# Four weight fusions in the opening of a gMLP and pooling backbone, with hand-placed side steps and four staging tiles

## The chip, the cores and the metric

The kernel runs on one core of a Trainium2 chip. The metric is device time in microseconds, from the first to the last instruction of the program and the little that lies around them; lower is better. Every program here is one launch, and all data starts and ends in the chip's main memory (HBM).

## The reference

Two layers work on 2048 latent tokens of width 1024, in float32. Each layer normalises its rows, scales and shifts them by an adaLN vector that is computed from a condition `c` and a weight `ada_w`, mixes them, and adds a gated residual. Layer 0 is a chunked gMLP, layer 1 a multi-scale centred pooling. Cut to what matters:

```python
shift, scale, gate = split(silu(c) @ ada_w[i] + ada_b[i], 3)
h = rmsnorm(x, norm_g[i]) * (1 + scale) + shift
# layer 0
u, v, g = split(h @ gmlp_w_in, 3)
s = einsum(w_s, layernorm(gelu(v))) + b_s        # over chunks of 128 tokens
y = (gelu(u) * s * silu(g)) @ gmlp_w_out
# layer 1
p, g = split(h @ pool_w_in, 2)
pooled = [centred_mean(p_k, w_k) - p_k for w_k in (2, 4, 8, 16)]
y = (einsum(pooled, pool_w_grp) * scale * silu(g)) @ pool_w_out
x = x + gate * y                                  # and a last rmsnorm
```

In layer 1 the pooling acts on tokens and `pool_w_grp` on channels, so the product of the first half of `pool_w_in` with `pool_w_grp` can be formed once, ahead of the rows. The kernel does so: this is the weight fusion, one 1024x512 product for each of the four windows (groups g = 0 to 3).

## The kernel before

Rows lie transposed (channels on partitions) in blocks of 512 tokens; two blocks make a pair. Big products use a seven-product scheme of the Strassen kind over quarters of weights and rows. Every float32 operand is split into a high and a low part (`put`, L108: a ScalarE copy for the high part, a VectorE subtraction for the low one), and each product is three matmuls (`mm3`, L102). One such split costs one instruction on each of the two engines.

Weights come through one stream (`Stream`, L33): a list of jobs, each with a load on SyncE's DMA queue into one of six `raw` tiles of 512 KB and a split. `st.get(i)` first issues loads for up to four jobs beyond the ones being split, and splits up to `st.ahead` jobs beyond i. The jobs are listed once at the start (L354 to L371), so their order in the list is the order of the loads.

The fusion of a group is `fuse(g)` (L705). It has two halves (kh), each with four steps (cc) of 12 matmuls into four accumulators `pf`; after each step it runs some steps of the side work. At the end of a half four copies on ScalarE (L716) bring the accumulators into staging tiles, and GpSimd's queue writes each to `wf_d` in HBM (L717), 256 KB a write. The staging tile is `t2`, a tag with two buffers, which the weight jobs also use for sums of quarters. The tag `s` has four buffers; its other users are the fourth quarter of the gMLP's v weights (`sixth`, L261), the gMLP's spatial results, and rows of the output phases.

The opening runs `fuse(0)`, `fuse(1)` and `fuse(2)`, and beside them a queue `side` of small steps: `ada`, ten steps that load eight rows of `ada_w` of 1 MB each (tag V, four buffers, of which one is the sum), accumulate them on VectorE (L446, L448), and end in small matmuls on TensorE (`pm`, L454) that give the scale and shift; `rs`, eleven steps that load the first 512 rows of x, square and sum them and end in their norm (`pss` L495, `pr` L519); `steps`, the same for the second 512 rows, which stay in eight of the nine `g` tiles; `halfs`, nine steps that modulate the first 512 rows and split them; and `late`, twelve steps that modulate the second 512 rows and form the sums of quarters that the seven products need, and four more (`late[1]`) for the last of these sums.

Side work is handed out by count: `do_side((2, 3, 3, 2)[g])` after each fusion step (L713). What is left after the third fusion runs in a loop of its own down to nine steps (L809), and the rest inside `v_phase(0)`, the first phase of the gMLP. `v_phase` takes its products in the order 1, 2, 6, 7, 5, 3, 4 (VORDER); 1 and 2 need the first 512 rows alone, 6 needs a sum from `late`. It hands out two side steps a slot in its first eight slots, in both calls (L859).

The fourth fusion, `fuse(3)`, runs later, between `b_phase0(0)` and `c_phase0(0)` (L1004), with the first nine steps of `sum_steps` (the rows of the next pair) beside it. In `v_phase(1)` the side work is `tsum`: for each of eight column blocks, reads of `wf_d` into x, x, ra and th, four VectorE sums (L736 to L739), and writes to `t_d`.

Instructions of an engine and of a DMA queue run in the order in which the program holds them; that order is made ahead of time by a planner that takes work whose buffers and inputs it expects to be ready, with the order of the source as priority. A `load` is held behind the last stream load that was listed before it (L127).

Of the kernel before, what the change touches and what calls it, by code (L numbers as in the profile page):

```python
# [22 lines left out]
TB = 512  # L23
# [40 lines left out]
def hybrid_kernel(ctx: ExitStack, tc: tile.TileContext, a: dict):  # L64
# [26 lines left out]
    def work(tag, width=512):  # L91
        return wk.tile([P, WK[tag][0]], F32, name=tag, tag=tag, bufs=WK[tag][1])[:, 0:width]
# [20 lines left out]
    side = deque()  # L113

    def do_side(n=1000):
        for _ in range(min(n, len(side))):
            side.popleft()()
# [110 lines left out]
    def fusion_jobs(g):  # L228
        rhs, lhs = [], [[], []]
        for kh in range(2):  # L230
            for cc in range(4):
                if kh == 0 and cc % 2 == 0:
                    rhs += halves(lambda cc=cc: a["pool_grp"][g, cc // 2], 512 if g == 0 and cc == 0 else W2)
                lhs[kh].append(half_job(lambda kh=kh, cc=cc: a["pool_wpT"][g, cc, :, kh * 512:kh * 512 + 512]))
        return rhs, lhs
# [115 lines left out]
            ws[1] += w(c, 1)  # L351
        return ys, ws

    jf = [fusion_jobs(g) for g in range(3)]  # L354
    jv, jug, jc0 = [], [], []
    for b in (0, 2):
        jv.append(v_jobs())
        jug.append(ug_jobs())
        if b == 0:
            jf.append(fusion_jobs(3))  # L360
        jc0 += [c0_jobs(b), c0_jobs(b + 1)]

    def pg_jobs():
# [167 lines left out]
    def src0(b):  # L531
        return lambda d: a["xT"][d, :, b * TB:(b + 1) * TB]
# [172 lines left out]
    def fuse(g):  # L705
        for kh in range(2):
            pf = [bank("pf") for _ in range(4)]
            for cc in range(4):
                x = st.get(rhs_lhs(g)[0][cc])
                w = st.get(rhs_lhs(g)[1][kh][cc])  # L710
                for k in range(4):
                    mm3(pf[k], part(w, every, slice(k * P, (k + 1) * P)), x, cc == 0, cc == 3)
                do_side((2, 3, 3, 2)[g])  # L713
            for kk in range(4):
                t = work("t2")
                nc.scalar.copy(t, pf[kk])  # L716
                nc.gpsimd.dma_start(  # L717
                    wf_d[(g % 2) * 4:(g % 2) * 4 + 4, kh, :, g // 2, kk, :].rearrange("j p n -> p j n"),
                    t.rearrange("p (j n) -> p j n", j=4))
# [31 lines left out]
    xbig, xb = [], []  # L751
# [9 lines left out]
    def bias_steps():  # L761
# [8 lines left out]
        def make(q):  # L770
# [4 lines left out]
            for i in range(2):  # L775
                for g in range(2):
# [11 lines left out]
    ada = ada_steps(0, 0, 16, lambda: bigtile("V", F32, "araw"), lambda: bigtile("V", F32, "aacc"))  # L788
    rs = rms0[0].steps(row_start)
    rows = Rows(0, [src0(0), src0(1)], rms0)  # L790
    others = []
    rms, steps = fetched_rms(src0(1), TB, "ra", "x", 2, others)
    rms0.append(rms)
    side.extend([ada[0], rs[0], rs[1], ada[1], rs[2], rest, ada[2], rs[3], rs[4], ada[3], rs[5], rest, ada[4], rs[6], rs[7], rest, ada[5],
                 rest, ada[6], rs[8], rest, ada[7], rs[9], rest, ada[8], rs[10], ada[9]])
    halfs = rows.half_steps(0, xb)
    two_ways = deque(steps)
    for f in halfs:
        side.append(f)
        for _ in range(2):  # L800
            if two_ways:
                side.append(two_ways.popleft())
    side.extend(two_ways)
    late = rows.rest_steps(xb, others)
    side.extend(late[0])

    for g in range(3):
        fuse(g)
    while len(side) > 9:  # L809
        do_side(1)  # L810


    def v_phase(pb, rows):

        st.ahead = 0
        bst = sp.tile([P, 8, 4, 6], F32, name="bst", tag="bst", bufs=1)

        def finish(i, n, t, src):

            nc.scalar.activation(t, src, AF.Gelu_apprx_tanh)  # L820
            nc.vector.bn_stats(bst[:, i, n, :], t)
            nc.gpsimd.dma_start(v_d[pb, 2 * n:2 * n + 2, :, i, :].rearrange("c p n -> p c n"),
                                t.rearrange("p (c n) -> p c n", c=2))

        for n in range(2):
            pa = [bank("pa") for _ in range(4)]
            pv = {}
            o = {}
            for pn in VORDER:
                idx, x = jv[pb][n][pn], rows.operand(NAME[pn])  # L830
                for t in range(4):
                    if pn in (1, 6, 7, 4):
                        p, onto = pa[t], pn != 1
                    else:
                        onto = pn == 3
                        if not onto:
                            pv[t] = bank("pv")
                        p = pv[t]
                    for k in range(4):
                        mm3(p, part(x[k], every, slice(t * P, (t + 1) * P)), st.get(idx[k]), k == 0, k == 3, onto)  # L840
                    st.make()
                    if pn in (1, 6, 5):
                        o[t, pn] = work("g")
                        nc.scalar.copy(o[t, pn], p)
                    elif pn == 2:
                        nc.vector.tensor_add(o[t, 1], o[t, 1], p)
                        finish(t, 2 * n, o[t, 1], o[t, 1])
                        if t == 3:
                            pv = {}
                    elif pn == 3:  # L850
                        nc.vector.tensor_add(o[t, 6], o[t, 6], p)
                        finish(t, 2 * n + 1, o[t, 6], o[t, 6])
                    elif pn == 4:
                        u = work("g")
                        finish(4 + t, 2 * n, u, p)
                    if pn == 5:
                        nc.vector.tensor_add(o[t, 5], o[t, 5], pa[t])
                        finish(4 + t, 2 * n + 1, o[t, 5], o[t, 5])
                    do_side(2 if n == 0 and pn < 3 else 1)  # L859
        mv = sp.tile([P, 8, 2], F32, name="mv", tag="mv", bufs=1)  # L860
        for i in range(8):
            nc.vector.bn_aggr(mv[:, i, :], bst[:, i].rearrange("p a b -> p (a b)"))
        ve, rs, rt, sh = (sp.tile([P, 8], F32, name=nm, tag=nm, bufs=1) for nm in ("ve", "rs", "rt", "sh"))
        nc.vector.tensor_scalar_add(ve, mv[:, :, 1], EPS)
        rsqrt(rs, ve, rt)
        nc.vector.scalar_tensor_tensor(sh, mv[:, :, 0], -1.0, rs, ALU.mult, ALU.mult)
        return mv, rs, sh
# [127 lines left out]
    for b in (2, 3):  # L995
        rms, steps = fetched_rms(src0(b), TB, "ra", "x", 5)
# [4 lines left out]
    rows = Rows(0, [src0(2), src0(3)], rms0)  # L1001
    sums = rows.sum_steps(lambda: work("g"))
    side.extend(sums[:9])
    fuse(3)  # L1004
    c_phase0(0)
    side.extend(sums[9:])
    c_phase0(1)
# [7 lines left out]
    for b in (0, 1):  # L1015
        rms, steps = fetched_rms(src1(b), TB, "ra", "x", 8)
# [4 lines left out]
    rows = Rows(1, [src1(0), src1(1)], rms1)  # L1021
# [115 lines left out]
    for b in (2, 3):  # L1137
        rms, steps = fetched_rms(src1(b), TB, "ra", "x", 8)
# [5 lines left out]
    rows = Rows(1, [src1(2), src1(3)], rms1)  # L1144
# [32 lines left out]
    for j, (t0, n) in enumerate(LAST):  # L1177
# [3 lines left out]
        rms = Rms(n, "ra", "x")  # L1181
# [79 lines left out]
```

## Time and profile before

| | us |
|---|---|
| median of three runs | 2511.09 |
| lowest and highest of them | 2510.03 and 2515.03 |
| the profiled execution | 2508.11 |
| its span | 2506.3 |

The rows below come from the one profiled execution. Times in them are microseconds from the start of its span. A timeline row gives the start, the length, the engine, the line and the operation with its tiles (written before, read behind the arrow); in brackets stands how long the engine was idle before it and what released it. PE is TensorE, PEld its weight loads, DVE VectorE, ACT ScalarE, POOL GpSimd, SPq the DMA queue of SyncE. The granted TensorE clock is given as a share of 2.4 GHz, so 0.50 is 1.2 GHz.

### The profile page before, as it was taken

The page shows a single profiled execution, that of the slowest core. Times are in us where ns is not written, and L with a number is a line of the kernel's source. Part 1 is how long each engine was busy: PE and PEld are TensorE (multiplying, and loading weights), DVE is VectorE, ACT ScalarE, POOL GpSimd, SP SyncE. Part 2 cuts the span into 40 slices and gives each one's busy share as a digit, 9 for nine tenths or more (in the row PEclk, how much of TensorE's full clock was granted, in tenths as well). Part 3 has the DMA queues.
Part 4 walks back from the last instruction along what each step waited for, and adds up shares of the span by engine and source line. Part 5 has one row for each costly group of instructions (what it writes and reads, how often), then busy time and mean ns, then how long its engine had stood idle before and what let it go on. Part 6 is the DMA issues. An engine that isn't in the chain of part 4 may idle for free.

```text
span 2506.3 us, 32884 instructions
## 1 busy us (share of the span) xinstructions
PE 2439.6 (97%) x11392; PEld 2054.6 (82%) x11392; DVE 1919.3 (77%) x3207; ACT 1038.4 (41%) x1833; POOL 258.7 (10%) x481
## 2 busy tenths in 40 slices
PE   6789999999999989999999999999999999999998
PEld 5668888888788878888888888888888888888998
DVE  5686788998854667888897737999885498999655
ACT  4554544333643434443335533333264333333533
POOL 2111100000100342000000001110000001010001
PEclk8799999999999999999999999999999999999999
DMA  9433434454755675343455645333367545354764
GB/s 351 162 114 120 152 113 139 154 168 137 247 192 187 213 251 183 113 130 123 137 160 189 216 158 172 125 110 113 108 211 230 161 138 189 117 168 136 251 194 146
DMA packets 170966, 418.43 MB, mean 167 GB/s; under 512 B 21408, under 2 KB 45984, under 8 KB 169776
## 3 DMA queue, kind: packets, MB, share of 16 engines
q1 hardware_dynamic: 138960, 314.01, 39.4%
q0 software_dynamic: 27808, 97.57, 10.7%
q10 hardware_dynamic: 4032, 4.75, 0.7%
q8 instruction: 90, 1.47, 0.2%
q14 instruction: 76, 0.62, 0.1%
HBM read 327.16 MB, written 89.10 MB: 166 GB/s over the span
## 4 chain that ended last, share of the span: by engine, by line
PE 61%; issue 23%; DVE 8%; DMA 5%; POOL 2%; ACT 1%; ACTq 0%; POOLq 0%; DVEq 0%; SPq 0%
PE pu L104 11%; PE pu L106 11%; PE pu L105 11%; PE po L104 6%; PE po L106 6%; PE po L105 6%; PE pa L104 2%; PE pa L105 2%; PE pa L106 2%; DVE wlo L111 1%; DMA wf_d<-t 1%; PE psp L899 1%; PE pv L105 1%; PE pv L106 1%; PE pv L104 1%
## 5 line engine op out<-in xcount | busy, mean ns | idle before, releaser
L111 DVE TENSOR_TENSOR wlo<-raw,whi 128x512 fp32r<-128x512 f32 x816 | 549.3, 685 | 266.6 <-ACT whi L110 261.0
L110 ACT CAST whi<-raw 128x512 fp32r<-128x512 f32 x816 | 489.0, 617 | 611.3 <-PE po L105 234.9
L104 PE MATMUL pu<-S,whi 128*128 128x512 f32 x1024 | 400.9, 391 | 0.0
L106 PE MATMUL pu<-S,wlo 128*128 128x512 f32 x1024 | 398.7, 389 | 0.0
L105 PE MATMUL pu<-S,whi 128*128 128x512 f32 x1024 | 398.5, 389 | 0.0
L106 PE MATMUL po<-whi,wlo 128*128 128x512 f32 (+1 forms) x768 | 300.1, 391 | 4.5 <-DVE wlo L111 4.5
L104 PE MATMUL po<-whi 128*128 128x512 f32 (+1 forms) x768 | 299.6, 390 | 1.2 <-ACT whi L110 1.2
L104 PE MATMUL pu<-A,whi 128*128 128x512 f32 x768 | 300.1, 391 | 0.0
L106 PE MATMUL pu<-A,wlo 128*128 128x512 f32 x768 | 299.1, 389 | 0.7 <-DVE wlo L111 0.7
L105 PE MATMUL po<-wlo,whi 128*128 128x512 f32 (+1 forms) x768 | 299.4, 390 | 0.0
L105 PE MATMUL pu<-A,whi 128*128 128x512 f32 x768 | 298.8, 389 | 0.0
L106 PEld LDWEIGHTS pu<-S,wlo 128*128 128x128 f32 x1024 | 192.2, 188 | 40.3
L105 PEld LDWEIGHTS pu<-S,whi 128*128 128x128 f32 x1024 | 192.3, 188 | 39.1
L104 PEld LDWEIGHTS pu<-S,whi 128*128 128x128 f32 x1024 | 192.3, 188 | 39.1
L106 PEld LDWEIGHTS po<-whi,wlo 128*128 128x128 f32 x768 | 144.6, 188 | 36.5 <-DVE wlo L111 6.5
L104 PEld LDWEIGHTS po<-whi 128*128 128x128 f32 x768 | 144.5, 188 | 32.0 <-ACT whi L110 1.8
L106 PEld LDWEIGHTS pu<-A,wlo 128*128 128x128 f32 x768 | 144.2, 188 | 31.3 <-DVE wlo L111 1.1
L105 PEld LDWEIGHTS po<-wlo,whi 128*128 128x128 f32 x768 | 144.5, 188 | 30.2
L104 PEld LDWEIGHTS pu<-A,whi 128*128 128x128 f32 x768 | 144.2, 188 | 29.8 <-ACT whi L110 0.4
L105 PEld LDWEIGHTS pu<-A,whi 128*128 128x128 f32 x768 | 144.2, 188 | 29.7
L105 PE MATMUL po<-big,whi 128*128 128x388 f32 (+1 forms) x384 | 123.1, 321 | 1.9 <-DVE big L111 1.9
L104 PE MATMUL po<-big,whi 128*128 128x388 f32 (+1 forms) x384 | 123.2, 321 | 0.0
(234 smaller groups left out, 4003.5 us busy)
## 6 DMA issues: line engine op xcount, KB each, us to landing
raw<-in_g_wo SPq DMA_DIRECT2D x64, 512.0 KB, 4.4
raw<-in_p_wo SPq DMA_DIRECT2D x96, 256.0 KB, 3.3
v_d<-g POOLq DMA_DIRECT2D x64, 256.0 KB, 2.7
raw<-in_g_wu SPq DMA_DIRECT2D x32, 512.0 KB, 4.0
raw<-in_g_wg SPq DMA_DIRECT2D x32, 512.0 KB, 4.5
raw<-v_d SPq DMA_DIRECT2D x32, 512.0 KB, 4.6
y_d<-s POOLq DMA_DIRECT2D x64, 256.0 KB, 2.7
x<-in_ada_w SPq DMA_DIRECT2D x64, 256.0 KB, 3.0
```

The lines of the kernel that those rows point to most:

```text
L104: nc.tensor.matmul(out, w[0], x[0], start=first and not onto, stop=False, skip_group_check=onto)
L105: nc.tensor.matmul(out, w[0], x[1], start=False, stop=False, skip_group_check=onto)
L106: nc.tensor.matmul(out, w[1], x[0], start=False, stop=last, skip_group_check=onto)
L110: nc.scalar.copy(pair[0], src)
L111: nc.vector.tensor_sub(pair[1], src, pair[0].bitcast(F32))
L899: nc.tensor.matmul(p[:, t * P:(t + 1) * P], vt[h][:, t * 2 * P + j * P:t * 2 * P + (j + 1) * P], bw[:, 0:P], start=True, stop=True)
```

## The change

All four fusions run in the opening, and their jobs stand ahead of everything else in the stream. The side work of the opening is no longer a queue with a count for each fusion but a table of 32 places, one for each fusion step; each side step is put in a place by hand. The staging tile of a fusion's result is `s` (four buffers) in place of `t2` (two). The loop that ran left-over side steps without products beside them is gone; the last three of the twelve `late` steps go to `v_phase(0)`. The pauses in the norm of the second 512 rows go (wait 2 becomes 0). In `v_phase` the pace of two steps a slot holds in the first call alone. `fuse(3)` is no longer between `b_phase0(0)` and `c_phase0(0)`, so the first nine `sum_steps` run inside `c_phase0(0)`.

```diff
-    jf = [fusion_jobs(g) for g in range(3)]
+    jf = [fusion_jobs(g) for g in range(4)]
...
-        if b == 0:
-            jf.append(fusion_jobs(3))
...
-                do_side((2, 3, 3, 2)[g])
+                for f in plan.pop(0):
+                    f()
             for kk in range(4):
-                t = work("t2")
+                t = work("s")
...
-    rms, steps = fetched_rms(src0(1), TB, "ra", "x", 2, others)
+    rms, steps = fetched_rms(src0(1), TB, "ra", "x", 0, others)
...
-    side.extend([ada[0], rs[0], rs[1], ada[1], rs[2], rest, ada[2], rs[3], rs[4], ada[3], rs[5], rest, ada[4], rs[6], rs[7], rest, ada[5],
-                 rest, ada[6], rs[8], rest, ada[7], rs[9], rest, ada[8], rs[10], ada[9]])
+    late = rows.rest_steps(xb, others)
     halfs = rows.half_steps(0, xb)
...
+    plan = [[] for _ in range(32)]
+
+    def place(steps, at):
+        for f, i in zip(steps, at):
+            plan[i].append(f)
+
+    place(rs, (0, 0, 1, 2, 3, 4, 5, 6, 10, 12, 13))
+    place(ada, (1, 2, 4, 6, 8, 10, 12, 14, 16, 18))
+    place(steps, (12, 14, 15, 16, 17, 18, 19, 20, 21, 24, 25, 26))
+    place(halfs, (18, 19, 19, 20, 20, 21, 21, 22, 22))
+    place(late[0], (27, 27, 28, 28, 29, 29, 30, 30, 31))
+    for g in range(4):
         fuse(g)
-    while len(side) > 9:
-        do_side(1)
+    side.extend(late[0][9:])
...
-                    do_side(2 if n == 0 and pn < 3 else 1)
+                    do_side(2 if pb == n == 0 and pn < 3 else 1)
...
     side.extend(sums[:9])
-    fuse(3)
     c_phase0(0)
```

## Rows read from the trace of the kernel before

**Rows 1.** The page: TensorE's busy time, its granted clock in 40 slices.

```profile
PE 2439.6 (97%) x11392; PEld 2054.6 (82%) x11392; DVE 1919.3 (77%) x3207; ACT 1038.4 (41%) x1833; POOL 258.7 (10%) x481
...
PEclk8799999999999999999999999999999999999999
```

**Rows 2.** Windows: length, busy time of each engine, clock, DMA share, GB/s.

```profile
0.00:69.00 69.00, 43.18 (x180) 33.66 (x180) 41.19 (x54) 27.32 (x49) 13.45 (x26) 0.85 0.95 350
20.00:40.00 20.00, 16.13 (x67) 11.87 (x65) 9.48 (x10) 7.14 (x13) 3.00 (x4) 0.96 1.02 399
0.00:152.00 152.00, 111.46 (x459) 89.36 (x460) 102.97 (x164) 78.81 (x140) 24.68 (x41) 0.85 0.62 220
```

**Rows 3.** Timeline of TensorE in the opening and the start of `v_phase(0)`.

```profile
7.38 0.69 PE L104 MATMUL pf<-whi 128*128 128x512 f32 x1 [0.35 <-ACT whi L110]
...
45.44 0.79 PE L104 MATMUL pf<-whi 128*128 128x512 f32 x1 [9.05 <-ACT whi L110]
...
69.18 6.99 PE L454 MATMUL pm<-ones,aacc 128*128 128x1 f32 x32 [10.83 <-DVE aacc L448]
...
111.83 0.39 PE L106 MATMUL pf<-whi,wlo 128*128 128x512 f32 x1
...
114.55 0.39 PE L106 MATMUL pa<-whi,A 128*128 128x512 f32 x1
122.18 1.22 PE L104 MATMUL pa<-whi,A 128*128 128x512 f32 x2 [7.24 <-ACT whi L110]
...
151.71 0.63 PE L104 MATMUL pa<-whi,S 128*128 128x512 f32 x1
```

**Rows 4.** Groups, 0 to 152: busy, mean ns, idle before, its releasers.

```profile
L448 DVE SCALAR_TENSOR_TENSOR aacc<-araw,cond,aacc 128x2048 f32<-128x2048 f32 x7 | 16.4, 2347 | 1.3 <-DMA araw<-in_ada_w 1.3
L716 ACT COPY t<-pf 128x512 f32<-128x512 f32 x24 | 14.0, 583 | 36.4 <-DMA wf_d<-t 30.9 <-PE pf L106 5.4
...
L105 PE MATMUL pv<-wlo,A 128*128 128x512 f32 x12 | 5.7, 475 | 7.3 <-DVE wlo L111 7.3
```

**Rows 5.** The tile wf_d, 0 to 140: landing times of its 24 writes.

```profile
DMA to landing us min/median/max: 2.7/6.3/8.6
```

**Rows 6.** DMA issues, 0 to 40: count, KB each, median us to landing.

```profile
araw<-in_ada_w SPq DMA_DIRECT2D x6, 1024.0 KB, 10.7
raw<-in_pool_wpT SPq DMA_DIRECT2D x15, 256.0 KB, 8.3
```

**Rows 7.** The chain that ended last: the small matmuls of a later adaLN part.

```profile
483.87 0.79 PE pm L454 x8
```

**Rows 8.** Timeline of VectorE: two subtractions and additions back to back.

```profile
118.70 0.68 DVE L582 TENSOR_TENSOR g<-g,rrow 128x512 f32<-128x512 f32 x1
119.30 0.68 DVE L643 TENSOR_TENSOR g<-g 128x512 f32<-128x512 f32 x1
```

**Rows 9.** Timeline around the fourth fusion: ScalarE, then TensorE.

```profile
652.59 0.59 ACT L716 COPY t<-pf 128x512 f32<-128x512 f32 x1 [2.37 <-DMA wf_d<-t]
656.53 1.22 PE L106 MATMUL po<-whi,wlo 128*128 128x512 f32 x2 [3.26 <-DVE wlo L111]
```

**Rows 10.** Windows: the fourth fusion's end, the start of `c_phase0(2)`.

```profile
650.00:660.00 10.00, 6.74 (x24) 5.13 (x23) 6.81 (x12) 6.52 (x13) 3.00 (x4) 0.83 0.67 234
1330.00:1340.00 10.00, 8.82 (x39) 6.84 (x38) 7.07 (x12) 4.47 (x8) 0.54 (x1) 1.00 0.56 147
```

**Rows 11.** Windows in `v_phase(1)`.

```profile
880.00:890.00 10.00, 7.79 (x35) 6.12 (x33) 2.77 (x4) 0.00 (x0) 4.33 (x8) 1.00 0.81 289
890.00:900.00 10.00, 5.29 (x12) 3.70 (x13) 6.99 (x12) 1.79 (x4) 4.00 (x7) 0.59 0.79 254
```

**Rows 12.** Timeline of VectorE in `v_phase(1)`.

```profile
891.55 0.69 DVE L736 TENSOR_TENSOR x<-x 128x512 f32<-128x512 f32 x1 [6.28 <-DMA x<-wf_d]
892.15 1.89 DVE L111 TENSOR_TENSOR wlo<-s,whi 128x512 fp32r<-128x512 f32 x3
```

**Rows 13.** Timeline of SyncE's DMA queue: two issues of adaLN rows.

```profile
38.04 9.65 SPq L128 DMA_DIRECT2D araw<-in_ada_w  x2
```

More of the change, by code (lines that the diff above doesn't have):

```diff
@@ L791, in hybrid_kernel @@
     others = []
-    rms, steps = fetched_rms(src0(1), TB, "ra", "x", 2, others)
+    rms, steps = fetched_rms(src0(1), TB, "ra", "x", 0, others)
     rms0.append(rms)
-    side.extend([ada[0], rs[0], rs[1], ada[1], rs[2], rest, ada[2], rs[3], rs[4], ada[3], rs[5], rest, ada[4], rs[6], rs[7], rest, ada[5],
-                 rest, ada[6], rs[8], rest, ada[7], rs[9], rest, ada[8], rs[10], ada[9]])
+    late = rows.rest_steps(xb, others)
     halfs = rows.half_steps(0, xb)
[L797 to L807, printed above, removed]
+    plan = [[] for _ in range(32)]
[8 more added lines that the diff above has]
+    for g in range(4):
         fuse(g)
-    while len(side) > 9:
-        do_side(1)
+    side.extend(late[0][9:])
     def v_phase(pb, rows):
```

## The prediction

> **What bounds the kernel now.** I read the page first: TensorE is busy for 97% of the span, and its granted clock is below full only in the first slices [rows 1]. So whatever moves the time has to give TensorE back time that it loses, and most of that is lost early. The windows of the opening come next [rows 2], then TensorE's timeline there [rows 3], and last the groups that say what ended the idle time of the other engines [rows 4].
>
> I set the mark at 151.71, where product 6 of `v_phase(0)` starts [rows 3]; until then TensorE should have done three fusions (288 matmuls) and products 1 and 2 (96). Twelve matmuls take 2.72 us from 111.83 to 114.55, 0.2267 us each [rows 3], so these 384 are worth 87.1 us. 151.7 - 87.1 = 64.6 us are spent otherwise. The first 7.4 are the start. The reader should see three kinds in the rest. First, TensorE waits 9.05 us for a weight's high part and later 7.24 us again [rows 3]: ScalarE, which makes these parts, stood in front of a copy L716 that waits for the write of an earlier result to leave its staging tile, 30.9 us in all [rows 4]. A write takes 6.3 us in the median and 8.6 at most [rows 5], and there are two tiles for four results. Second, 10.83 us for the sum of the adaLN rows; the small matmuls `pm` behind it then take 6.99 us, because the clock had fallen (the same kind takes 0.79 us for 8 records at full clock, so 3.2 for 32) [rows 3, 7]. Third, VectorE is late when `v_phase(0)` begins: 7.3 us of waits for low parts in product 2 [rows 4]. After the mark TensorE runs without a gap for a long while.
>
> **The change part by part.** *The fourth fusion moves.* Its 96 matmuls (21.8 us) leave the middle and come before the mark; TensorE's work is the same. With it move 12 splits, 3 MB of loads on SyncE's queue (they no longer stand ahead of the first loads of `c_phase0(0)`), and 8 writes on GpSimd's. Like for like, the mark before counts as 151.7 + 21.8 = 173.5.
>
> *The floors of the new opening.* TensorE: 7.4 + 480 x 0.2267 = 116.2, plus `pm` at full clock 3.2 and the norm's small matmuls, for which I take as much again, 122.6 us. VectorE: 103.0 busy until the mark [rows 2], plus 12 splits at 0.60, the distance of two starts [rows 8]: 110.2; it begins near 6, so 116. DMA: 220 GB/s for 152 us are 33.4 MB [rows 2]; with 5 MB (5.2 million bytes) more, 38.7 MB; at the 399 GB/s of the fullest stretch [rows 2] 97 us. All three lie near each other: the gain is what the order saves of the waits, and the new mark can't come before about 123.
>
> *Four staging tiles.* A half of a fusion lasts 48 x 0.2267 = 10.9 us. Its four writes are out some 4 us after its end and land in 6.3 to 8.6 [rows 5], at 10 to 13 us; the next half asks for the first tile at 11 and for the last at 13. So the copy's wait falls to between 0 and 1 us; I take 0. The `s` loads of v weights (1 MB) now wait for the last writes of the fusion, until 10 to 13 us after its end; with a landing like the other weights' 8.3 us at worst [rows 6] they are there at 18 to 21, and product 6 starts at 21.8 and wants four VectorE operations (2.4 us) first. Cost 0 to 2, I take 0; no load for products 1 and 2 stands behind them on SyncE's queue.
>
> *The adaLN rows in places 1 to 18.* The last one's load is issued at place 14. Ahead of it in the queue I count 7.75 MB of fusion weights, 2.5 of x, 8 of `ada_w` (sizes as in [rows 6]) and 3 of written results: 21.25 MB, 22.3 million bytes. At 399 GB/s and a start at 2.5 us they have landed at 58.4, at the 350 of the first 69 us [rows 2] at 63.7. One accumulation of 2.35 us follows [rows 4]: 60.7 to 66.0. TensorE reaches the `pm` of place 18 at 7.4 + 19 x 2.72 + 1.7 = 60.8. So it waits 0 to 5 us; I take 4, nearer to the slower end, since that row is the same stretch with its start, and 1 to 2 more for a clock that then falls: 5. The Trainium skill (DMA: Bandwidth & Descriptors, Specifications) gives about 358 GB/s as the HBM limit of a core. By it the wait would be some 4 us; the row with 399 goes above that figure, so I keep the two rows as bounds.
>
> *Fusion loads behind them.* Each raw load is needed 4 to 6 places (11 to 16 us) after its issue, and loads take 8.3 to 10.7 us in this stretch [rows 6]. That is just enough; 0 to 10 us, I take 4.
>
> *VectorE at the start of `v_phase(0)`.* Nine of twelve `late` steps are now done or queued before it, where nine were left. But from place 19 on VectorE has some 41 us of work (12 splits and 4 ahead, `halfs`, the second norm, nine `late` steps, at 0.60 each) for 37 us of products, and then three `late` steps, `late[1]` and the sums for product 6. The wait was 7.3 [rows 4], some 10 with the slow restarts; 0 to 10, I take 6. Small gaps between steps and at the norm's matmuls: 2 to 6, I take 4.
>
> New mark: 122.6 + 0 + 5 + 4 + 6 + 4 = 141.6. Gain 173.5 - 141.6 = 31.9 us.
>
> *The middle.* The fourth fusion ended in a stop of 3.26 us, behind the same kind of copy, which waited 2.37 us [rows 9]; 24 matmul records in ten us where full stretches have 46 are 22 x 0.2267 = 5.0 us [rows 10]. It goes. `c_phase0(0)` then begins with nine `sum_steps` beside it, as `c_phase0(2)` does now, which loses 7 records, 1.6 us [rows 10]. Gain 3.4.
>
> *Pace in `v_phase(1)`.* 11 and 34 records are missing there, 10 us [rows 11]: sums of fused weights stand on VectorE ahead of splits and wait 6.28 us for their reads of `wf_d` [rows 12]. The new pace spreads these steps by source order. In the second half the pace was one already, with 19 us from one set of sums to the next, and yet they come 10 to 12 us apart; the planner runs ahead of the places. I take 0 here, bounds 0 and 10 gained.
>
> Sum: 31.9 + 3.4 = 35.3 us off the profiled execution's 2508.1, 2472.8. The median of the runs lies 3.0 above that execution, so 2476.
>
> **The rivals.** (a) *The stop in `v_phase(1)` goes too*, because the pace holds the sums back. For it speaks that four places lie between reads and sums, 10.9 us, more than the reads need; against it the planner's habit above. 2476 - 10 = 2466. (b) *The transfers take the place of the staging wait.* DMA share is 0.95 for the first 69 us [rows 2]; if `pm` and the fusion weights come at the slow ends (5 + 2 and 10) and VectorE is as late as before (10), the mark is near 154 and the time 2488. The Trainium skill (same page, Issuing engines are not separate DMA queues) says that DMAs of all queues interleave on the same 16 engines; by that rule four writes in flight slow the loads beside them, which is this rival's mechanism, and the 6.3 us of a write [rows 5] beside 8.3 of an equal load [rows 6] agrees. (c) *Near the floor*: waits of 6 in all, mark 129, 2463, with (a) 2453. (d) *Slower*: SyncE's queue holds. Two adaLN issues took 9.65 us at its head [rows 13], and fusion loads stood behind them. In the new opening five of these rows (the fourth to the eighth) must wait for one of three buffers; if each holds the queue for 10 us, 50 us, of which six raw tiles cover some 13, 37 us are lost: the gain of 35 is gone and with slow restarts the time is about 2517. It decides from a hold of about two places (5.4 us) for each row. Against it: the accumulations that free the buffers are two places apart, and the copies no longer stop the engines that feed them. (e) *It doesn't do what it says*: planner and queues keep the order much as it was, the waits stay and the time is within 5 us of 2511.
>
> **How the numbers follow.** Forecast 2476, its own range 2468 to 2485: 0.48. (a) 0.19, (b) 0.17, (c) 0.07, (d) 0.05, (e) 0.04. The range for 8 in 10 reaches from 2456, below (a) and the upper part of (c), to 2494, above (b). About 0.2%, 5 us, is what a measurement of this kernel can tell from no change. Faster: 0.91; the same: 0.04; slower: 0.05.
>
> **What would show it.** Right: no copy L716 waits over 1 us for `wf_d`; `pm` starts between 61 and 68, at 3 to 5 us length; four fusions end near 110; product 6 starts near 142; no stop at the start of `c_phase0(0)` over 2 us; the stop near 880 to 900 there as before, some 35 us earlier in the span. Wrong: `pm` after 72, or a mark after 155 (transfers or VectorE are the new bound), or weight loads that land over 12 us after issue while TensorE waits for high parts; and a `v_phase(1)` without its stop would show (a).

## The result and the profile after

| | before | after |
|---|---|---|
| median of four runs, us | 2511.27 | 2481.93 |
| lowest and highest | 2510.03 and 2515.03 | 2480.48 and 2483.58 |
| span of the profiled execution | 2506.3 | 2480.4 |

The ratio is 0.9881, with a 95% interval of 0.9864 to 0.9898: 29.3 us off by the medians, 25.9 by the two profiled spans (the profiled execution of before, 2508.11, lay 3.2 under its median, that of after, 2482.26, 0.3 above its own). The forecast was 2476 in a range of 2456 to 2494.

The page of after, TensorE, VectorE and ScalarE, and the clock in 40 slices:

```profile
PE 2436.2 (98%) x11392; PEld 2050.5 (83%) x11392; DVE 1918.4 (77%) x3207; ACT 1037.0 (42%) x1833; POOL 261.1 (11%) x481
...
PEclk9999999999999999999999999999999999999999
```

The work is the same as in [rows 1]; the dent of the clock in the second slice has gone. The windows of after (length, busy time of PE, PEld, DVE, ACT and POOL with instructions, clock, DMA share, GB/s) answer to [rows 2]:

```profile
0.00:69.00 69.00, 60.77 (x262) 49.86 (x263) 47.29 (x66) 34.42 (x61) 18.57 (x30) 0.95 0.95 356
10.00:40.00 30.00, 27.14 (x115) 22.04 (x114) 20.21 (x25) 16.86 (x31) 6.63 (x8) 0.94 1.01 376
0.00:152.00 152.00, 136.97 (x589) 110.70 (x590) 115.93 (x187) 92.07 (x162) 34.35 (x52) 0.94 0.72 258
70.00:80.00 10.00, 9.69 (x46) 8.68 (x47) 4.78 (x9) 3.94 (x8) 0.21 (x1) 0.69 0.84 289
146.00:156.00 10.00, 8.09 (x33) 5.48 (x31) 10.00 (x23) 2.44 (x4) 3.41 (x6) 0.99 0.36 121
155.00:165.00 10.00, 9.62 (x34) 7.16 (x35) 8.69 (x20) 4.24 (x8) 2.01 (x4) 0.83 0.33 107
```

In the first 69 us TensorE runs 262 matmuls where it ran 180. The DMA share was 0.95 and is 0.95: the same full pipe now feeds more products. TensorE's timeline in the opening of after answers to [rows 3]:

```profile
37.12 0.79 PE L104 MATMUL pf<-whi 128*128 128x512 f32 x1 [2.87 <-ACT whi L110]
...
71.59 4.79 PE L452 MATMUL pm<-ones,aacc 128*128 128x1 f32 x32
...
118.33 0.39 PE L104 MATMUL pa<-whi,A 128*128 128x512 f32 x1
...
138.69 0.50 PE L105 MATMUL pv<-wlo,A 128*128 128x512 f32 x1 [1.22 <-DVE wlo L111]
143.50 0.50 PE L104 MATMUL pv<-whi,A 128*128 128x512 f32 x1 [3.16 <-DVE g L846]
146.35 0.61 PE L104 MATMUL pa<-whi,S 128*128 128x512 f32 x2
154.94 1.41 PE L104 MATMUL pa<-whi,S 128*128 128x512 f32 x4 [1.91 <-ACT whi L110]
174.27 0.39 PE L104 MATMUL pv<-whi,S 128*128 128x512 f32 x1
```

`pa<-whi,A` at 118.33 is the first row of `v_phase(0)`, `pa<-whi,S` at 146.35 the start of its product 6, `pv<-whi,S` at 174.27 that of product 5. The stops of 9.05, 10.83 and 7.24 us are gone; the longest that is left is 3.16. Before `pm` stands no wait: its sum was there, but only just. The last accumulation, on VectorE, ended at 71.28:

```profile
68.93 2.35 DVE L446 SCALAR_TENSOR_TENSOR aacc<-araw,cond,aacc 128x2048 f32<-128x2048 f32 x1
```

ScalarE's groups in 0 to 170 (busy, mean ns, idle before and its releasers) answer to [rows 4]; the splits of weights of before, in 0 to 152, follow:

```profile
L110 ACT CAST whi<-raw 128x512 fp32r<-128x512 f32 x64 | 38.0, 625 | 22.7 <-DMA raw<-in_pool_wpT 14.7 <-DMA raw<-in_pool_grp 5.5 <-DVE raw L278 1.4
L715 ACT COPY s<-pf 128x512 f32<-128x512 f32 x32 | 17.5, 590 | 10.9 <-PE pf L106 9.3 <-DMA wf_d<-s 1.4
```

```profile
L110 ACT CAST whi<-raw 128x512 fp32r<-128x512 f32 x44 | 25.8, 618 | 2.6 <-DMA raw<-in_pool_wpT 1.4 <-DMA raw<-in_pool_grp 0.7 <-PE pf L105 0.3
```

The copies' wait for `wf_d` fell from 30.9 us [rows 4] to 1.4, and ScalarE's wait for raw weights rose from 2.1 to 20.2. So the engine does not stand less by 29.5 us; for a part it stands for something else. TensorE's waits for high parts in 0 to 170 fell from 16.6 us to 7.9.

*The mark.* The next three rows are TensorE's timeline of before, behind the row at 151.71 on which the sum set its mark [rows 3].

```profile
152.14 0.65 PE L104 MATMUL pv<-whi,A 128*128 128x512 f32 x1
156.06 0.39 PE L105 MATMUL pa<-wlo,S 128*128 128x512 f32 x1
...
178.99 0.39 PE L104 MATMUL pv<-whi,S 128*128 128x512 f32 x1
```

One matmul of product 6 had been put ahead; at 152.14 product 2 goes on (`pv<-whi,A`), and product 6 proper runs from 156.06. Like for like, with 21.8 us for the fourth fusion, that is 177.8 against 146.35 after: 31.5 us gained, where 31.9 were forecast.

*Given back in products 6 and 7.* From there to product 5 TensorE took 22.9 us before (178.99 - 156.06) and 27.9 after (174.27 - 146.35); 96 matmuls at the 0.2267 us of the forecast are 21.8. The net gain of the opening is 178.99 + 21.77 - 174.27 = 26.5. The window 146 to 156 shows VectorE full and 33 matmuls where a full window counts 46. The stop of 1.91 us at 154.94 is for a high part, and ScalarE, which makes it, stood before it at a gelu that waits for VectorE:

```profile
153.67 0.63 ACT L820 ACTIVATE g<-g 128x512 f32<-128x512 f32 x1 [4.45 <-DVE g L846]
```

*The middle.* The stop behind the fourth fusion [rows 9] is gone and `c_phase0(0)` starts with one short wait:

```profile
627.03 0.50 PE L104 MATMUL po<-whi 128*128 128x512 f32 x1 [1.15 <-ACT whi L110]
```

Starts of the same products stand 26.48 us apart at 625 (like for like) and 29.83 at the start of `v_phase(1)`: 3.35 gained.

*`v_phase(1)`.* Windows of after, then VectorE's timeline there; they answer to [rows 11, 12].

```profile
850.00:860.00 10.00, 7.95 (x36) 6.25 (x34) 3.28 (x5) 0.00 (x0) 4.33 (x8) 1.00 0.68 228
860.00:870.00 10.00, 6.00 (x13) 4.30 (x14) 6.88 (x11) 2.51 (x5) 4.05 (x8) 0.61 0.79 271
870.00:880.00 10.00, 8.48 (x32) 6.50 (x31) 7.64 (x13) 3.51 (x7) 5.70 (x10) 0.87 0.76 234
...
910.00:920.00 10.00, 8.03 (x33) 5.76 (x33) 6.79 (x12) 1.77 (x3) 2.15 (x4) 1.00 0.36 129
```

```profile
851.03 0.69 DVE L735 TENSOR_TENSOR x<-x 128x512 f32<-128x512 f32 x1 [7.70 <-DMA x<-wf_d]
860.66 0.69 DVE L735 TENSOR_TENSOR x<-x 128x512 f32<-128x512 f32 x1 [6.28 <-DMA x<-wf_d]
```

The same stop has more parts now: against 46 a window, 70 records are missing in these four, where 45 were in the two of before [rows 11]. The gain falls from 29.83 at the start of the phase to 25.15 behind it: 4.7 us lost. By the starts of the products the first stop, 850 to 880, costs only 0.8 us more than that of before; 3.0 go in the product that runs from 912.77 to 926.62.

### The profile page after: what moved, and what is told of

The parts are those of the page before. It is cut to its first block, busy times and chain, and to the rows that moved or that the text cites. A ratio compares the mean times of both kernels' runs of the same rounds, so it can differ in the third digit from the quotient of the medians.

```text
span 2480.4 us, 32891 instructions
## 1 busy us (share of the span) xinstructions
PE 2436.2 (98%) x11392; PEld 2050.5 (83%) x11392; DVE 1918.4 (77%) x3207; ACT 1037.0 (42%) x1833; POOL 261.1 (11%) x481
## 4 chain that ended last, share of the span: by engine, by line
PE 71%; issue 14%; DVE 6%; DMA 6%; POOL 2%; ACT 1%; ACTq 0%; SPq 0%; POOLq 0%; DVEq 0%
PE pu L104 14%; PE pu L106 14%; PE pu L105 14%; PE po L104 7%; PE po L105 7%; PE po L106 7%; PE psp L899 2%; DVE wlo L111 1%; PE pa L105 1%; PE pa L104 1%; PE pa L106 1%; DMA raw<-in_pool_wpT 1%; DMA th<-wf_d 1%; PE pv L104 1%; PE pv L105 1%
```

## The experiments

All medians are set beside the kernel before on the same chip (2512.38, 2512.31, 2512.88 and 2509.65 us in the four sets). These medians of one kernel lie up to 3.2 us apart, so a difference to the changed kernel that is no larger is not told apart from none. "Product 5" is TensorE's first row of that product in `v_phase(0)`: 178.99 before, 174.27 after.

### The staging tile: taken back, and alone

The changed kernel with `t2` again, and the kernel before with `s` and nothing else of the change:

```diff
-                t = work("s")
+                t = work("t2")
```

> The changed kernel with its fusion results staged in t2 (two buffers) again; everything else as changed. Theory A (the staging tile is what paid): ScalarE's copies wait for their writes again, some 20 to 30 us in all in the opening, TensorE's waits for high parts come back, 2495 to 2502 us. Theory B (the places and the move paid; a wait for the staging tile only takes the turn of waits for weights and for VectorE, which are there anyway): 2482 to 2488 us.

> The kernel before with nothing but the staging tile changed, t2 to s; three fusions in the opening, side work by count, the fourth fusion in the middle. Theory A: the waits of 9.05 and 7.24 us on TensorE go with their slow restarts, and the stop of 5 us at the end of the fourth fusion; 2490 to 2497 us. Theory B: in the opening the sum of the adaLN rows and VectorE are as late as before, only the stop in the middle goes; 2503 to 2508 us.

With `t2` again: 2501.80 us, ratio 0.9957 (0.9942 to 0.9972), 19.9 above the changed kernel and within theory A. ScalarE's copies in 0 to 170, and TensorE's longest wait there (total, times, longest):

```profile
L715 ACT COPY t<-pf 128x512 f32<-128x512 f32 x32 | 18.3, 585 | 55.8 <-DMA wf_d<-t 40.6 <-issue 8.1 <-PE pf L106 7.1
```

```profile
PE pf L104 <- ACT whi L110: 18.6, 3, 9.6
```

The wait is back, 40.6 us for 32 copies, and behind it TensorE waits 18.6 us for high parts. With `s` alone: 2497.27 us, ratio 0.9938 (0.9920 to 0.9956), 15.1 below the kernel before; in the opening the copies wait for hardly anything but TensorE:

```profile
L716 ACT COPY s<-pf 128x512 f32<-128x512 f32 x24 | 13.1, 588 | 3.7 <-PE pf L106 3.5
```

Product 5 starts at 163.87 there, 15.1 earlier, and the time lies 0.3 us above the end of theory A's 2490 to 2497. (That both are 15.1 is chance: by the profiled spans this run is 8.9 us shorter, since 3.2 us of the gain are lost again ahead of `v_phase(1)` and 3.7 in it.) One part of that theory failed: the stop at the end of the fourth fusion, in the middle, did not go with the tile. The copies of that fusion (590 to 690) wait there too, since the tag `s` also holds rows that go to `y_d`:

```profile
L716 ACT COPY s<-pf 128x512 f32<-128x512 f32 x8 | 4.6, 584 | 5.5 <-DMA y_d<-s 3.4 <-DMA wf_d<-s 1.8 <-PE pf L106 0.3
```

TensorE's longest wait there is 2.7 us, where it was 3.3 in the kernel before, and in `no_move` below, where both theories held that it does not come back, it is 2.5. In the middle the move took the stop away, not the tile. The tile carries the larger part of the gain from either side: 15 us alone, 20 with the rest around it. For the opening the step "wait 0" is shown.

### The move and the places

`s_and_move` is the kernel before with `s` and all four fusions in the opening, the side work still handed out by count. `no_move` is the changed kernel with the fourth fusion back in the middle, these lines reversed; what stood in places 24 to 31 is handed out by count.

```diff
-    jf = [fusion_jobs(g) for g in range(3)]
+    jf = [fusion_jobs(g) for g in range(4)]
...
-    for g in range(3):
+    for g in range(4):
         fuse(g)
...
-    fuse(3)
     c_phase0(0)
```

> The kernel before with staging in s and all four fusions in the opening, but side work handed out by count (2, 3, 3, 2) and no places by hand. Theory A: nearly all of the gain, 2483 to 2488 us. Theory B: without places the adaLN rows are as dense as before and TensorE waits for their sum some 10 us; 2492 to 2500 us.

> The changed kernel with the fourth fusion back between b_phase0(0) and c_phase0(0); three fusions, the first 24 places as changed, what stood in places 24 to 31 is handed out as in the kernel before; staging in s. Both theories hold that the stop at the end of the fourth fusion does not come back, as its copies find free tiles. Theory A: the opening lacks 22 us of products to lie beside VectorE's and ScalarE's work, so that part of it stands bare: 2490 to 2496 us. Theory B, in which the places alone pay: 2480 to 2486 us.

`s_and_move`: 2485.32 us (2481.50 to 2487.41), ratio 0.9889 (0.9871 to 0.9908). `no_move`: 2490.75 us (2487.50 to 2495.79), ratio 0.9914 (0.9894 to 0.9935). Both lie within theory A. So the steps are, one after the other: tile 15.1, move 12.0, places and the rest 3.4 us; the last is not told apart from none, since the intervals of `s_and_move` and the changed kernel overlap. Taken away from the whole, the move is 8.8. In the trace the places bring more early: product 5 is at 180.62 without them and at 174.27 with them, 6.4 us, of which some is lost again in `v_phase(1)`. `pm` waits 8.3 us for its sum in `s_and_move` as it does in `s_alone`, and not at all in the changed kernel: that is what places 1 to 18 took away.

### The adaLN rows

Seven of the eight rows of `ada_w` are not loaded (the first stands for all, so scale and shift are not the reference's).

```diff
+        kept = []
...
+            if ng == 16 and k:
+                return kept[0]
             r = raw()[:, 0:ng * P]
+            kept.append(r)
```

> The changed kernel with one of the eight adaLN rows of the opening loaded and used eight times, so 7 MB, 18 to 20 us of transfers at 365 to 400 GB/s, are left out; the scale and shift of layer 0 are not the reference's. All engine work stays. Theory A (transfers hold the first half of the opening, then ScalarE and VectorE the second): the waits of TensorE before 72 us go, the fusions end at 108 to 113 in place of 118.3, and part of that is lost again before product 5; 2474 to 2479 us. Rival B (transfers bind all of it): 10 us or more, below 2472. Rival C (VectorE alone binds): 2480 to 2484 us.

2468.44 us (2466.54 to 2472.29), ratio 0.9829 (0.9814 to 0.9844): 13.5 us below the changed kernel, which is rival B's side. The first 69 us, and TensorE's wait for high parts in 0 to 170:

```profile
0.00:69.00 69.00, 63.94 (x304) 54.20 (x305) 51.75 (x72) 38.45 (x70) 16.89 (x30) 1.00 0.87 302
```

```profile
PE pf L104 <- ACT whi L110: 0.6, 1, 0.6
```

TensorE fits 304 matmuls where the changed kernel has 262, the wait of 5.6 us is 0.6, `v_phase(0)` starts at 106.63 in place of 118.33 and product 5 is 11.1 us earlier. With 7 MB less in the pipe the products run nearly at TensorE's pace: in the first half of the new opening the transfers are the bound. (The edit takes the seven issues out of SyncE's queue as well as the bytes; it is the DMA share of 1.01 in 10 to 40 us that speaks for the bytes.) Theory A's loss ahead of product 5 did not come: of 11.7 us at the start of `v_phase(0)` 11.1 are left there.

### VectorE where `v_phase(0)` begins

`less_vector` leaves out the twelve VectorE operations that rebuild the difference for the fourth sum (the operand S4 is then not the reference's):

```diff
-                t, u = work("g"), work("g")
...
-                    nc.vector.tensor_add(x, hi.bitcast(F32), lo.bitcast(F32))
-                nc.vector.tensor_sub(t, t, u)
-                put(self.quarter("S4", k), t)
+                put(self.quarter("S4", k), self.quarter("S2", k)[0].bitcast(F32))
```

`adds_on_gpsimd` keeps them, and puts eight of them on GpSimd:

```diff
-                    nc.vector.tensor_add(x, hi.bitcast(F32), lo.bitcast(F32))
+                    nc.gpsimd.tensor_add(x, hi.bitcast(F32), lo.bitcast(F32))
```

> The changed kernel without the three VectorE operations in each of the four late[1] steps that form the last sum of quarters (its split reads a part that is there), 12 operations, 7.2 us of VectorE at the start of v_phase(0); that operand is not the reference's. Theory A (VectorE's backlog makes the waits in products 2, 6 and 7, some 12 us in all): product 5 starts 5 to 7 us earlier, 2474 to 2478 us. Rival B (the v weights that wait for the staging tiles of the last fusion, or ScalarE, make them): 2480 to 2484 us.

> The changed kernel with the eight additions that rebuild two operands in the last side steps of v_phase(0) on GpSimd in place of VectorE; the result is the same. Theory A (the 5 us lost in products 6 and 7 are VectorE's backlog, and leaving twelve operations out gave more than they cost because VectorE is full there): eight of those twelve go from VectorE, some two thirds of the 10.9 us: 2473 to 2478, product 5 at 167 to 170 (174.27 in the changed kernel). Rival B (GpSimd takes 1.3 to 1.5 us for each where VectorE takes 0.6, the subtraction on VectorE waits for it and stands ahead of splits): 2479 to 2485, with waits of VectorE for GpSimd's tiles.

Without the twelve: 2471.06 us (2466.61 to 2475.72), ratio 0.9838 (0.9820 to 0.9856), 10.9 below the changed kernel and below theory A's 2474 to 2478. TensorE's timeline there:

```profile
137.33 0.39 PE L104 MATMUL pa<-whi,S 128*128 128x512 f32 x1
140.46 0.39 PE L105 MATMUL pa<-wlo,S 128*128 128x512 f32 x1
...
165.15 0.39 PE L104 MATMUL pv<-whi,S 128*128 128x512 f32 x1
```

Product 5 comes 9.1 us earlier, for 12 x 0.60 = 7.2 us of VectorE. The start of `v_phase(0)` is only 1.1 us earlier (117.23), so the rest comes from products 1, 2, 6 and 7: VectorE's backlog is the bound there, and taking its operations out gave more than they last. The clock fits that: it is 0.83 in the window 155 to 165 of after, behind the stop of 1.91 us, and TensorE pays for the restart too. The edit also takes away eight `g` tiles and ScalarE's wait of 5.9 us for the difference that it splits; what VectorE's time alone is worth is not told apart from these.

Moved to GpSimd the work gains nothing: 2483.60 us (2482.12 to 2488.27), ratio 0.9886 (0.9867 to 0.9905), product 5 at 175.08. GpSimd's timeline, VectorE's beside it, the longest wait of ScalarE in 110 to 176, and TensorE's longest in 118 to 176:

```profile
118.81 6.98 POOL L655 TENSOR_TENSOR g<-A,A 128x512 f32<-128x512 f32 x1
125.76 1.28 POOL L655 TENSOR_TENSOR g<-S,S 128x512 f32<-128x512 f32 x1
```

```profile
127.07 1.76 DVE L656 TENSOR_TENSOR g<-g 128x512 f32<-128x512 f32 x1 [2.43 <-POOL g L655]
128.75 1.75 DVE L111 TENSOR_TENSOR wlo<-raw,whi 128x512 fp32r<-128x512 f32 x1
...
132.12 0.68 DVE L656 TENSOR_TENSOR g<-g 128x512 f32<-128x512 f32 x1
```

```profile
ACT S L110 <- DVE g L656: 12.3, 4, 4.8
```

```profile
PE pv L105 <- DVE wlo L111: 6.2, 2, 3.6
```

The additions take 1.28 to 1.72 us and the first shows 6.98 (POOL's spans are rough), while VectorE works without a gap to 124.64. VectorE comes out no lighter: four of its operations that lie beside GpSimd's take 1.75 to 1.77 us where one with GpSimd quiet takes 0.68, and a row of five at 137.41 takes 5.29, where 3.1 are usual. That is some 6.5 us more, against the 8 x 0.60 = 4.8 that were taken off. To this come waits: VectorE's subtraction waits 2.43 us for GpSimd, and ScalarE stands 12.3 us in front of the split of S4, waiting for such subtractions; in the changed kernel that is 5.9 us. TensorE waits 6.2 us for low parts of weights, which stand behind all this on VectorE, where it waited 1.2. Rival B held by its time, but it had only the waits; that VectorE's own operations get longer was in neither theory, and which of the two cost more is not told apart.

### The pace and the sums in `v_phase(1)`

`old_pace` gives the second call its two steps a slot again. `sums_on_gpsimd` leaves the pace and takes the four sums from VectorE:

```diff
-                    do_side(2 if pb == n == 0 and pn < 3 else 1)
+                    do_side(2 if n == 0 and pn < 3 else 1)
```

```diff
-            nc.vector.tensor_sub(b11, b12, b11)
+            nc.gpsimd.tensor_sub(b11, b12, b11)
...
```

> The changed kernel with the pace of two side steps a slot back in the first eight slots of v_phase(1). Theory A (the new pace itself made the stops there worse, by some 20 matmuls, 4.5 us): 53 missing matmuls there again, 2476 to 2479 us. Theory B (the planner orders these sums by when it expects their reads, the pace hardly matters): within 2 us of the changed kernel, 2480 to 2484 us.

> The changed kernel with the four sums of each column block in v_phase(1) on GpSimd in place of VectorE. Theory A (VectorE stands at these sums while their reads are under way, and the splits and statistics behind them are what TensorE waits for): the stops of 13 and 3 us in v_phase(1) go, 2464 to 2470 us. Rival B (GpSimd takes over 2 us for each sum and stands at the waits itself, with writes of v behind it, so that v_phase(1) stops for free g tiles): 2478 to 2492 us.

`old_pace`: 2479.00 us (2476.40 to 2483.80), ratio 0.9871 (0.9855 to 0.9888). Its interval overlaps that of the changed kernel, so the times alone don't settle it; in the trace the phase loses 0.8 us (a gain of 28.35 at its start and of 27.60 behind it) where the changed kernel loses 4.7. The stop is still there, with 8 records in 860 to 870.

`sums_on_gpsimd`: 2481.46 us (2481.07 to 2485.09), ratio 0.9884 (0.9867 to 0.9900): no gain. Its windows, and two waits in 860 to 960:

```profile
850.00:860.00 10.00, 10.00 (x46) 8.29 (x45) 6.74 (x11) 6.34 (x12) 7.55 (x10) 1.00 0.66 217
860.00:870.00 10.00, 10.00 (x46) 8.29 (x45) 9.21 (x13) 4.55 (x8) 7.66 (x9) 1.00 0.62 233
...
890.00:900.00 10.00, 5.29 (x15) 3.00 (x14) 10.00 (x11) 3.83 (x7) 9.56 (x12) 0.77 0.49 174
...
910.00:920.00 10.00, 7.24 (x24) 5.25 (x23) 8.57 (x10) 2.96 (x6) 8.21 (x12) 0.83 0.72 227
```

```profile
ACT g L820 <- DMA v_d<-g: 19.5, 3, 16.7
...
ACT g L844 <- DMA v_d<-g: 9.4, 3, 3.2
```

The first stop is gone (850 to 870 are full), and product 4 of the first half starts at 868.72, 11.4 us earlier than in the changed kernel. Then it is lost again: GpSimd now stands in front of its reads, the writes of `v_d` stand behind it on the same queue, their `g` tiles don't come free, and ScalarE waits 16.7 us for one. The wait had changed its engine, not its harm.

### A wait without followers

If the wait harms only through what is queued behind it, it should cost nothing on a queue that holds nothing else that TensorE needs. Both of these have the sums on GpSimd and the `v_d` writes of the second call issued by ScalarE (and, here, the additions of above too); the second has the old pace as well.

```diff
-            nc.gpsimd.dma_start(v_d[pb, 2 * n:2 * n + 2, :, i, :]...
+            (nc.scalar if pb else nc.gpsimd).dma_start(v_d[pb, 2 * n:2 * n + 2, :, i, :]...
```

> As the run before, and also the four sums of fused weights on GpSimd and, in the second v_phase, the writes to v_d issued by ScalarE in place of GpSimd, so that nothing that TensorE needs stands behind GpSimd's wait for its reads. Theory A (the stop in the second v_phase is a queue that waits for reads of wf_d, first VectorE's, then GpSimd's with the writes behind it; freed of followers the wait costs nothing): 8 to 11 us below the run before, 2463 to 2470, no window of ten us with under 36 matmul records between 850 and 930. Rival B (TensorE is short there of splits or of transfers anyway, so the loss only changes its place): within 3 us of the run before, and thin windows still there.

> As the run before, with the pace of before (two steps a slot in the second v_phase's first eight slots too). Theory A (the pace matters only through the reads that VectorE or GpSimd wait for; with the wait harmless it is worth nothing): within 2 us of the run before. Rival B (the earlier reads and sums themselves keep some us, as they seemed to with the sums on VectorE, 2.9 us by the medians): 2 to 4 us below the run before.

2472.80 us (2469.30 to 2479.78), ratio 0.9844 (0.9817 to 0.9871), and 2472.55 us (2469.81 to 2476.39), ratio 0.9840 (0.9821 to 0.9858). Against `adds_on_gpsimd` the first is 10.8 us lower, as theory A had it, though above its 2463 to 2470 since the additions gave nothing, and the pace is worth nothing any more. The first one's trace has no thin window from 850 to 930, and one stop behind that, in the windows and on ScalarE:

```profile
930.00:940.00 10.00, 6.01 (x25) 4.71 (x24) 5.08 (x8) 5.05 (x9) 0.00 (x0) 0.91 0.45 116
940.00:950.00 10.00, 10.00 (x35) 7.93 (x35) 8.10 (x14) 7.23 (x13) 0.00 (x0) 0.75 0.46 146
```

```profile
932.25 0.63 ACT L481 ACTIVATE ra<-x 128x512 f32<-128x512 f32 x1 [17.73 <-DMA t_d<-ra]
```

The sums run later on GpSimd, and the first square of the next norm, which uses the same tile `ra`, was ordered into ScalarE's queue before they were done. It holds the splits behind it for 17.73 us.

The last run takes that away: the square is held behind the phase's last gelu, and the additions are on VectorE again.

```diff
-            if d == 0 or kept is not None:
+            if d == 0 and after is not None:
+                with tc.issue_after(after):
+                    rms.square(x, True)
+            elif d == 0 or kept is not None:
                 rms.square(x, d == 0)
...
```

> The changed kernel with the four sums of fused weights on GpSimd and the v_d writes of the second v_phase issued by ScalarE, without the additions on GpSimd, and with the first square of the next norm held behind the phase's last gelu on ScalarE. In the run with both, that square stood on ScalarE at 917 to 935 waiting for the tile ra, which the sums still used, and 7 us were lost there after 11 had been gained. Theory A (that stop is the square's wait alone): the 7 us stay, 2463 to 2469, no window of ten us under 40 matmul records between 840 and 950. Rival B (the reads of the next rows and the weights behind them on SyncE's queue, or VectorE behind ScalarE, hold TensorE at the same place anyway): 2470 to 2474, with thin windows near 930 to 950 or at the start of the next phase.

2465.49 us (2459.97 to 2467.71), ratio 0.9816 (0.9799 to 0.9833): 44.2 us below the kernel before, and 16.4 below the changed kernel by the medians (14.8 when each is set beside its own before). Its page and the same two windows:

```profile
PE 2431.8 (99%) x11392; PEld 2049.6 (83%) x11392; DVE 1918.0 (78%) x3175; ACT 1041.6 (42%) x1833; POOL 278.7 (11%) x481
```

```profile
930.00:940.00 10.00, 10.00 (x46) 8.29 (x45) 7.83 (x13) 7.14 (x14) 0.00 (x0) 1.00 0.19 60
940.00:950.00 10.00, 10.00 (x46) 8.29 (x45) 9.86 (x20) 4.12 (x8) 0.00 (x0) 1.00 0.68 229
```

All windows from 830 to 970 are full, with 45 records or more. The loss in `v_phase(1)` was a matter of who stands behind a waiting instruction, on three engines in turn; the transfers and the splits were there in time for all of it. That it was the wait and not VectorE's work one sees in the stop itself, where VectorE is busy for 3.28 of 10 us (850 to 860 of after).

## Why the prediction was right, and where it was off

| step | forecast, us | measured, us |
|---|---|---|
| `v_phase(0)` starts (116.2 - 21.8 + 6.4 + 13) | 113.8 | 118.33 |
| products 1 and 2, with VectorE's 6 | 27.8 | 28.0 |
| product 6 starts, after | 141.6 | 146.35 |
| the same of before, like for like | 173.5 | 177.8 |
| gain to there | 31.9 | 31.5 |
| products 6 and 7 | 0 | -5.0 |
| the middle | 3.4 | 3.35 |
| `v_phase(1)` | 0 | -4.7 |
| sum, by the profiled spans | 35.3 | 25.9 |

In the first row 116.2 is TensorE's floor with products 1 and 2 in it (21.8), 6.4 the small matmuls and 13 the waits. The rows from the gain on add up to 25.2; the last 0.7 are spread over the rest.

*What held.* The mechanism, the direction and the two largest terms: the staging wait of the opening ends with four tiles (shown from both sides), products 1 and 2 lose the 6 us given to VectorE, `pm` lasts 4.79 us where 3 to 5 were said, the middle gives 3.35 for 3.4. Rivals (d) and (e) did not come: TensorE's waits for parts of fusion weights were 8.2 us in all, not 37, and the waits of before did not stay. Nor did (c): the mark did not come near 129.

*The mark.* The opening's 31.9 came out at 31.5 because two errors of the same size cancelled. Before, one matmul that the planner had put ahead was taken for a product's start (151.71 for 156.06, 4.4 us). After, the fusions ended 4.5 us later than the sum said. The check for the first would have been the next row: a product's start is the row from which its kind goes on.

*The adaLN rows and the fusion loads.* The step gave 5 to `pm` and its clock, 4 to the loads and 4 to small gaps. `pm` came at 71.59, outside 61 to 68, and yet without a wait, because both sides were late. TensorE had waited for high and low parts of weights (3.8 and 2.6 us up to there). And the sum came 5.3 us behind its slow bound of 66.0: the last row of `ada_w` was issued at 52.67, took 15.6 us to land, and its accumulation ended at 71.28. A TensorE at its forecast 60.8 would have waited some 10 us; that no wait shows is luck. The clock cost more than the 1 to 2 us given: `pm` 1.6 over its 3.2, and behind it the matmuls came 0.43 us apart from 76.81 to 80.65, nine of them, 1.8 us more, with 0.69 granted in 70 to 80. `one_ada_row` shows the cause: rival (b)'s mechanism, transfers in place of the staging wait, was there (20.2 us of ScalarE's waits in place of 2.1), at some 11 us of TensorE's time; but rival (b)'s mark, near 154, was not reached. The forecast took the two as exclusive, and they were not.

*The signs.* Of those named ahead, the copies' wait (0.8 us at most), the length of `pm` and the start of `c_phase0(0)` came; `pm`'s start, the end of the fusions (118.3 for 110) and product 6 (146.35 for 142) came late. One sign of being wrong came in part: in the first 72 us loads of fusion weights landed after 9.9 us in the median and 15.8 at most, while TensorE waited for high parts, though the load behind its longest wait there (2.87 us) landed after 10.2.

*"After the mark TensorE runs without a gap for a long while."* This was read from before and carried over to after without a price. The nine `late` steps ahead of `v_phase(0)` left three, `late[1]`, the sums for product 6 and the gelu's steps behind its start, and VectorE did not catch up within products 1 and 2, as the 6 us assumed. `less_vector` shows that the backlog reached on to product 5. The step that failed is the mark itself: a term for a busy engine was closed where the sum ended, while the engine was still full.

*Pace in `v_phase(1)`.* The sum took 0 with bounds of 0 to 10 gained, and no loss. Measured were 4.7 us lost. The new order of the reads made the waits in front of VectorE longer (7.70 and 6.28 us where the row of before has 6.28), and the bounds should have reached below nothing, since the operations' order was changed and nothing in the trace excluded a loss. How much of the 4.7 is the pace's stays open: 3.9 us by the trace of `old_pace`, not told apart from 0 by the times. Rival (a) did not come; what it was worth was 10 us and more, and the last run had it.

Of the 9.4 us by which the spans missed, 5.0 and 4.7 are these two steps. The median missed by 5.9 only, and that by chance: the forecast added 3.0 us because the profiled execution of before lay below its median, and that of after did not.

## What to carry to other kernels

Count a staging tile by the time until its write has landed, not until it is issued: with fewer tiles than results in flight, the engine that copies stands, and all that it feeds stands behind it. A wait costs what is queued behind it on its engine; before work is moved to a free engine, look at what that engine's queue holds, at who uses the same tiles next, and at whether the engine that it leaves slows down beside it. And carry a sum on to the point where the busiest engine has a gap again, since a term closed at a mark in the middle of a backlog is given back behind it.

## What the runs showed of the hardware

A float32 subtraction of 128x512 took 1.29 to 1.55 us in the mean on GpSimd (by its four lines, in `sums_on_gpsimd`) where VectorE starts one every 0.60 [rows 8]. The Trainium skill (Trainium Architecture — The Big Picture, The five engines, in one table) calls GpSimd two times slower than VectorE in streaming elementwise work; the runs here show 2.1 to 2.6 times. Four of VectorE's operations on such tiles took 1.75 to 1.77 us beside GpSimd's additions, where 0.68 is their length else (in `adds_on_gpsimd`, 127 to 135). The issue of the same `v_d` write took 0.37 us on ScalarE and 0.72 in the mean on GpSimd. In the opening the 16 DMA engines moved 376 GB/s over 10 to 40 us at a share of 1.01, and with four writes in flight a write of 256 KB landed after 6.5 us in the median and 11.2 at most, where two in flight had 6.3 and 8.6 [rows 5]; the estimate of 6.3 to 8.6 in the forecast was short by that, and the copies still waited 1.4 us only. In the 32 one-column matmuls of `pm`, which TensorE reached without a wait, the granted clock fell all the same: it was 0.50 (1.2 GHz) in 76 to 80 and 1.00 in 82 to 84.
